# One layer of an RWKV-7 and neighbourhood-attention backbone: a gate's matmuls moved into the fourth inverse's first steps, residual halves of w_out and m made by adding DMAs, and the first half's sums written ahead of the second modulation

## The chip, the cores and the metric

The kernel runs on one core of a Trainium2 chip. The metric is the device time of one execution in microseconds (us). Engines are named as the profile names them: PE is the matrix engine (PEld its weight loads), DVE the vector engine, ACT the scalar engine, POOL the general engine, SP the engine that issues most DMAs.

## What is computed

640 tokens (128 of a prompt, 512 of a latent grid) go through one layer of width 1024. The lines that matter here are

```python
o_rw, s_new = _rwkv_branch(...)      # 8 heads, forward and backward, gated state recurrence
o_na = _na_context(q, k, v)  or  _na_latent(q, k, v, ctx_k, ctx_v, p["na_rpb"])
merged = (jax.nn.sigmoid(gate_rw) * (o_rw @ p["w_o_rwkv"])
          + jax.nn.sigmoid(gate_na) * (o_na @ p["w_o_na"]))
x = x + g1 * (merged @ p["w_out"])
h2 = _rmsnorm(x, p["norm2_g"]) * (1.0 + sc2) + sh2
x = x + g2 * ((jax.nn.silu(h2 @ p["ffn_w1"]) * (h2 @ p["ffn_w3"])) @ p["ffn_w2"])
```

All of it is in float32 accuracy. The kernel gets it by splitting each operand of the large matmuls into a high part `hi` (rounded to the PE's fast 32-bit form) and a residual `lo` (value minus `hi`), and adding three products: hi by hi, lo by hi, hi by lo.

## The kernel before

The layer is one stream in time. First come the norm and the modulation vectors, then the projections, the neighbourhood attention, the RWKV recurrence, the merge, `w_out`, and from about 745 us to the end the feed-forward part (FFN).

**The recurrence** works in four groups of chunks, `ct` = 0 to 3. Each group has four stages: `main`, `inv`, `carry` and `out`. `inv(ct, S)` (L1253) inverts 32 by 32 triangles on DVE in 30 steps `s` (L1274 for the first three, then a product L1288 and a sum L1292, each in two halves). After certain steps it calls jobs: `PRM["jobs"][ct]` names the steps after which `v_job` (L1211, small transposes of v), `t_job` (L1234) and `g_job` (L1183, L1186, small products) are put on PE, each job for a part of the chunks' slots. A `g_job` leaves a closure `masks`, which multiplies its results by a triangular mask on DVE (L1195 into `AG`, L1198 into `TG`); `PRM["mds"][ct]` names the steps after which the closures run. All these small products, and those of the bonus term (`bonus`: L1103, L1117, L1132 on PE; L1107, L1134, L1439, L1440, L1443 on DVE), write into one rotating pool of six PSUM banks named `w`. A product that opens a bank waits until whoever read the bank's previous tenant has finished.

**The fill.** The recurrence alone leaves PE idle, so `weave` (L1552) pulls matmuls of another stream, `stream(PRM["order"])`, between the steps. The first number of each entry of `PRM["plan"]` says how many of the stream's matmuls follow a step; the other two advance `out` of the group before and `bonus`. In the inverse of ct=3 the stream has reached the last gate, g14 (L572, tiles `h` times a gate weight, `fl`), and then a0, the first products with the recurrence's outputs of earlier groups, whose operands `o` come back from DRAM by eight DMAs at L1476 (320 KB each, `o<-o_d`). Gate weights come by DMA from SP (`wst`, L164 or L167) and are split by `wcast`: ACT casts `hi` (L177); `lo` is made either by DVE (L179, `wst - hi`) or, for the tiles marked so, by ACT writing minus the rounded value into `lo` (L175) and POOL issuing a DMA that adds `wst` to it (L176, an adding or accumulating DMA).

**The merge and w_out.** `last_gen` (L1634) makes the merged `m`, 8 blocks of 128 columns in 2 halves of 320 tokens, 16 halves in all. Each takes three matmuls (L1644), a DVE operation that combines them with the gate (L1645, reading PSUM), a DVE sum with the other branch (L1647), an ACT cast to `mh` (L1648) and a POOL subtraction to `ml` (L1649). From the sixth half on, two matmuls of `w_out`'s first half of columns (`w_out_gen`, L288, results `acc`) follow each half, and the rest are drained after the last.

**After w_out's first half.** `add_gated` (L1680) multiplies `acc` by the gate row `G` (L1683, result `tt`) and adds it to the residual `x2` (L1684), for five token tiles. The second modulation turns two rows into columns by 16 tiny matmuls (`pc`, L1704) and three small DVE operations (L1706 to L1708). Then PE runs w_out's second half of columns (L288 again); its weights' `lo` parts are DVE's L179.

Inside the regions marked manual the order of an engine is the order of the code; PE is manual throughout the part around `last_gen`, the other engines are not there, and a scheduler at build time fixes their order.

Of the kernel before, what the change touches and what calls it, by code (L numbers as in the profile page):

```python
# [14 lines left out]
P = 128  # L15
# [34 lines left out]
        ("0.0.0 16.1.0 8.1.1 9.0.0 2.1.0 8.1.1 13.1.1 0.1.1 0.1.1 0.1.1 0.1.0 6.1.0 6.1.0 6.1.0 6.1.0 "  # L50
         "6.1.0 6.1.0 7.1.0 6.0.0 6.0.0 6.0.0 6.0.0 6.0.0 6.0.0 7.0.0 6.0.0 6.0.0 6.0.0 6.0.0 6.0.0 "
         "6.0.0 6.0.0 11.0.0 8.0.0 8.0.0 2.0.0 0.0.0"),
# [15 lines left out]
        "w >hb >lb",  # L68
        ""),
    fp=(6, 12, 18), h2e="dpddddpddd", x0e="a", ze="aa", y2=1, y1=0, sc=3, sr=3, sp=1, mg=1.915, h1=0.952,  # L70
    h2=0.91, jobs=((2, 9, 28), (2, 9, 28), (2, 9, 28), (2, 8, 28)),
    mds=((4, 12), (4, 12), (4, 12), (4, 12)), bud=((1.8, 0.8), (1.3, 1.8)), off=6, tk=2, h3=1,
    h4=1.07, g1=2, km="dddddddd", kb="ddpd", ma="d", yo="pppd", r0="pd", rl=(0, 0, 0), lh=(0, 0, 1, 1),
    wl="dddddddddppppppppppppppppppppppppppdddd", nu=9, lg=14, jo=(2, 0, 1), na=(
        "6.0.12.0.1 6.0.12.0.0 6.0.12.0.0 6.0.12.0.2 6.0.12.0.0 6.0.12.0.2 6.0.12.0.0 6.0.12.0.2 6.0.12.0.0 "
        "6.0.12.0.2 6.0.12.1.0 6.1.12.1.2 6.2.12.2.0 6.1.12.2.2 6.0.12.2.0 6.1.12.1.2 6.2.14.2.0 "
        "6.2.14.1.2 6.2.14.2.0 6.2.14.2.0 6.3.18.2.0 10.0.10.0.0"))
# [30 lines left out]
def body(ctx: ExitStack, tc: tile.TileContext, xs, xp, cols, consts, w_ada, b_row, w_rw, w_qkv,  # L108
# [73 lines left out]
    def wload(src, eng=None):  # L182
        return wcast(wdma(src), eng)
# [307 lines left out]
    pend, off, hold = [], [0], [False]  # L491
# [580 lines left out]
    with ExitStack() as s3:  # L1072
# [500 lines left out]
        with tc.manual_schedule(engines=FIRST):  # L1573
            for d in range(2):
                akr(S, d)
            pool.memset(Nt, 0.0)
            og = iter(())
            for ct in range(4):
                bg = bonus(ct, S)
                weave(main(ct, S), (og,))  # L1580
                if ct == 0:
                    for d in range(2):
                        r_(S, d, dve)
                    pool.memset(Rt, 0.0)
                marks.add(f"A{ct}")
                S2 = Ct()
                if ct < 3:
                    prep_dma(ct + 1, S2, sb.tile([P, NT], F32, tag="mx", bufs=2, name=nm("upw")))
                weave(inv(ct, S), (og, bg))
                drain(og)  # L1590
                marks.add(f"I{ct}")
                if ct < 3:
                    need(f"k{ct + 1}")
                    prep_cast(S2)
                    pg = prep(ct + 1, S2)
                else:
# [24 lines left out]
                hold[0] = True  # L1621
                weave(carry(ct, S, last), (pg,), PRM["bud"])
                hold[0] = False
                og = out(ct, S)
                S = S2
            weave(og)
            need(*(f"b{i}" for i in range(4)))
            c0 = wload(w_out[0])


    pp = open_pool(ctx, "pp4", bufs=3, space=PSUM)
# [1 line left out]
    mh, ml = hilo("m")  # L1633
    def last_gen():  # L1634
        ts_ = []
        for c8 in range(8):
            t = pre_t() if c8 < 4 else trp.tile([P, NT], F32, tag="tr", bufs=4, name=nm("tr"))
            sp.dma_start(t, trw_d[c8])
            ts_.append(t)
        for c8, t in enumerate(ts_):  # L1640
            for (a, b) in halves:
                ps = pp.tile([P, 512], F32, tag="tp", name=nm("fl"))
                for n, (w, x) in enumerate(((wo[0], o3[0]), (wo[0], o3[1]), (wo[1], o3[0]))):
                    pe.matmul(ps[:, :H2], w[:, c8 * 128:c8 * 128 + 128], x[:, a:b], start=n == 0, stop=n == 2)  # L1644
                dve.scalar_tensor_tensor(out=t[:, a:b], in0=t[:, a:b], scalar=1.0, in1=ps[:, :H2],  # L1645
                                         op0=ALU.add, op1=ALU.mult)
                dve.tensor_tensor(out=t[:, a:b], in0=mt[c8][:, a:b], in1=t[:, a:b], op=ALU.add)  # L1647
                act.copy(mh[:, c8, a:b], t[:, a:b])  # L1648
                pool.tensor_tensor(out=ml[:, c8, a:b], in0=t[:, a:b], in1=mh[:, c8, a:b].bitcast(F32),  # L1649
                                   op=ALU.subtract)  # L1650
                yield

    def w_out_gen(pss, ws, toks, **kw):
        return tok_gen(pss, pp, (mh, ml), ws, list(range(8)), toks, **kw)

    pss = {}
    trp = open_pool(hs, "trp")
    weights(hs, 2, 2)
    w0 = w_out_gen(pss, [c0] + [w_out[q] for q in range(1, 4)], range(5))
# [5 lines left out]
    hs.close()  # L1665
    nstack.close()
    xpool = open_pool(ctx, "xpool")
    x2 = [xpool.tile([P, 1024], F32, name=f"x2_{i}") for i in range(5)]
    G = xpool.tile([P, 2, 1024], F32, name="G")
    m2 = xpool.tile([P, 24, 2], F32, name="m2")[:, 0:8, :]  # L1670
    s2 = xpool.tile([P, 8, 2], F32, name="s2")
    for i in range(5):
        sp.dma_start(x2[i], xs[i * 128:(i + 1) * 128, :] if i < 4 else xp)

    def load_gate(b):
        ad = adr[:, :]
# [32 lines left out]
    for i in range(5):  # L1709
        add_gated(pss[i], i, 0, 0.5)  # L1710


    nr = [{} for _ in range(5)]
# [372 lines left out]
```

## Time and profile before

| | |
|---|---|
| median of 3 runs | 1182.05 us (1181.28 to 1182.42) |
| profiled execution | 1182.22 us, of it span 1180.4 us |
| granted PE clock, mean | 0.99 |
| PE busy | 1123.0 us, 95% of the span |
| DVE, ACT, POOL busy | 777.8, 531.6, 192.1 us |
| DMA moved | 148.11 MB, mean 125 GB/s |

The span is the time between the first and the last recorded instruction; 1.8 us of the execution lie around it. A row of the timeline gives the start, the time until the row's last instruction ended, engine, line, operation, output and input tiles, and in square brackets the idle time ahead of it and what ended that.

### The profile page before, as it was taken

To read this page: it belongs to the slowest core of one execution; us is meant where nothing else is said; L and a number is where in the kernel's file an instruction comes from. 1 tells how busy PE (TensorE), PEld (TensorE's weight loads), DVE (VectorE), ACT (ScalarE), POOL (GpSimd) and SP (SyncE) were. 2 spreads that over 40 slices of the span, in tenths; PEclk is the share of its full clock that TensorE was granted. 3 is DMA by queue.
4 is the path that set the end of the run, shared out by engine and by line. 5 is a ranking of instruction groups with operands and counts; after the bars stand their busy time and mean duration, and the time that the engine had idled before them with its cause. 6 is when DMAs were issued, how large, how long until landed. Compare 5 with 4: busy or idle time off the path is not lost.

```text
span 1180.4 us, 26871 instructions
## 1 busy us (share of the span) xinstructions
PE 1123.0 (95%) x11160; PEld 995.3 (84%) x11160; DVE 777.8 (66%) x1635; ACT 531.6 (45%) x1050; POOL 192.1 (16%) x260
## 2 busy tenths in 40 slices
PE   6999999899999999999799899999999999999998
PEld 4688877789888988888698777899899989998997
DVE  4565465559558747936486756887568757775775
ACT  4444656554564665556343323554124422441330
POOL 1162244320101202111100141100000000001000
PEclk9999999999999999999899999999999999999999
DMA  9752777654433523433753641312312231232122
GB/s 334 261 116 86 240 224 227 208 137 109 104 83 93 138 69 91 112 102 95 241 151 102 223 161 54 108 54 90 107 54 90 79 101 55 89 107 90 54 79 101
DMA packets 60194, 148.11 MB, mean 125 GB/s; under 512 B 7428, under 2 KB 22404, under 8 KB 60072
## 3 DMA queue, kind: packets, MB, share of 16 engines
q1 hardware_dynamic: 55464, 131.56, 34.1%
q0 software_dynamic: 3744, 13.63, 5.9%
q8 instruction: 88, 1.44, 0.5%
q10 hardware_dynamic: 864, 1.20, 0.3%
q14 instruction: 34, 0.28, 0.1%
HBM read 118.41 MB, written 14.32 MB: 112 GB/s over the span
## 4 chain that ended last, share of the span: by engine, by line
PE 62%; DVE 9%; ACT 3%; issue 3%; DMA 1%; SPq 0%; POOL 0%; DVEq 0%; ACTq 0%; POOLq 0%
PE f L1805 21%; PE acc L288 16%; PE fl L201 12%; PE w L1362 1%; PE w L1389 1%; DVE pr L1288 1%; PE w L1402 1%; DMA o<-o_d 1%; PE w L1374 1%; PE mm L201 1%; PE w L1186 1%; DVE RL L1292 1%; PE w L1380 1%; PE w L1419 1%; PE w L1234 1%
## 5 line engine op out<-in xcount | busy, mean ns | idle before, releaser
L1805 PE MATMUL f<-t,whi 128*128 128x320 f32 x640 | 141.8, 310 | 0.0
L1805 PE MATMUL f<-b,whi 128*128 128x320 f32 x608 | 136.2, 311 | 2.0 <-ACT b L189 1.7
L288 PE MATMUL acc<-whi,u 128*128 128x512 f32 (+1 forms) x448 | 136.0, 385 | 0.0
L201 PE MATMUL fl<-h,whi 128*128 128x320 f32 x672 | 121.2, 320 | 1.3 <-issue 1.3
L177 ACT CAST whi<-wst 128x1024 fp32r<-128x1024 f32 (+1 forms) x77 | 79.2, 1033 | 63.6 <-PE acc L288 43.0
L1805 PEld LDWEIGHTS f<-t,whi 128*128 128x128 f32 x640 | 107.3, 189 | 0.0
L201 PEld LDWEIGHTS fl<-h,whi 128*128 128x128 f32 x672 | 101.4, 188 | 6.1 <-issue 1.4
L1805 PEld LDWEIGHTS f<-b,whi 128*128 128x128 f32 x608 | 102.3, 189 | 3.2 <-ACT b L189 2.1
L1805 PE MATMUL f<-t,wlo 128*128 128x320 f32 x320 | 99.1, 310 | 0.0
L288 PEld LDWEIGHTS acc<-whi,u 128*128 128x128 f32 x448 | 83.5, 188 | 16.6
L1805 PE MATMUL f<-b,wlo 128*128 128x320 f32 x304 | 94.6, 311 | 2.2 <-DVE wlo L1849 2.2
L1846 ACT CAST whi<-ws 128x1024 fp32r<-128x1024 f32 x40 | 42.0, 1051 | 108.7 <-PE f L1805 47.5
L179 DVE TENSOR_TENSOR wlo<-wst,whi 128x1024 fp32r<-128x1024 f32 (+1 forms) x51 | 62.2, 1227 | 38.1 <-ACT whi L177 37.5
L288 PE MATMUL acc<-wlo,u 128*128 128x512 f32 (+1 forms) x224 | 86.3, 385 | 0.0
L1860 POOL TENSOR_TENSOR ws<-wst 128x512 f32<-128x512 f32 x20 | 28.1, 1405 | 340.7 <-DVE wlo L1849 226.7
L288 PE MATMUL acc<-whi,h 128*128 128x512 f32 x240 | 78.1, 399 | 0.9 <-DVE h L413 0.9
L201 PE MATMUL fl<-h,wlo 128*128 128x320 f32 x336 | 63.4, 321 | 0.0
L1683 DVE SCALAR_TENSOR_TENSOR tt<-acc,G 128x512 f32<-128x512 f32 (+1 forms) x51 | 34.5, 679 | 42.8 <-PE acc L288 42.7
L1846 ACT CAST whi<-wst 128x1024 fp32r<-128x1024 f32 (+1 forms) x48 | 41.4, 870 | 42.3 <-PE acc L288 37.6
L1805 PEld LDWEIGHTS f<-t,wlo 128*128 128x128 f32 x320 | 60.2, 188 | 0.0
L1805 PEld LDWEIGHTS f<-b,wlo 128*128 128x128 f32 x304 | 57.5, 189 | 2.5 <-DVE wlo L1849 2.5
L1849 DVE TENSOR_TENSOR wlo<-ws,whi 128x1024 fp32r<-128x1024 f32 x40 | 54.9, 1372 | 6.3 <-ACT whi L1846 6.3
(342 smaller groups left out, 2503.7 us busy)
## 6 DMA issues: line engine op xcount, KB each, us to landing
wst<-in_w_dram SPq DMA_DIRECT2D x66, 512.0 KB
wst<-in_w_rw_dram SPq DMA_DIRECT2D x31, 512.0 KB
wlo<-wst POOLq DMA_DIRECT2D x26, 512.0 KB, 4.6
wa<-in_w_ada_dram SPq DMA_DIRECT2D x24, 512.0 KB
f<-in_w_ada_dram SPq DMA_DIRECT2D x16, 512.0 KB
wst<-in_w_qkv_dram SPq DMA_DIRECT2D x12, 512.0 KB
o<-o_d SPq DMA_DIRECT2D x14, 320.0 KB
x<-in_xs_dram SPq DMA_DIRECT2D x8, 512.0 KB
```

The costliest lines, as they stand in the source:

```text
L177: act.copy(hi[:, :n], st[:, :n])
L179: dve.tensor_tensor(out=lo[:, :n], in0=st[:, :n], in1=hi[:, :n].bitcast(F32), op=ALU.subtract)
L201: pe.matmul(ps[:, :t1 - t0], w[:, a:a + 128], x[:, k0 + kt, t0:t1], start=n == 0, stop=n == 3 * nk - 1)
L288: pe.matmul(pss[i][:, a:b], lhs(x, kt, ts_), w[:, cs_], start=ki == 0 and n == 0, stop=ki == last and n == 2)
L1186: pe.matmul(pr[h][hrows[h ^ i], o_], x[hrows[h], :], R_[hrows[h], l, :], start=True, stop=True)
L1234: pe.matmul(pt[h][hrows[h ^ i], o_], S.BK[l // 10][hrows[h], l % 10, i, :], idh(h), start=True, stop=True)
L1288: dve.tensor_tensor(out=prv, in0=V(RL[:, s + 1 + a, :], [[32, b - a], [0, s]], s), in1=V(RL[:, s, :], [[0, b - a], [1, s]]), op=ALU.mult)
L1683: dve.scalar_tensor_tensor(out=tt, in0=ps[:, a:b], scalar=c, in1=G[:, g, sl], op0=ALU.mult, op1=ALU.mult)
L1805: pe.matmul(ps[:, :H2], w_[:, c_], x_[:, kt, :], start=first and kt + n == 0, stop=last and kt == 3 and n == 2, skip_group_check=more)
L1846: act.copy(r[0][:, :width], src())
L1849: dve.tensor_tensor(out=r[1][:, :width], in0=src(), in1=r[0][:, :width].bitcast(F32), op=ALU.subtract)
L1860: eng_x(PRM["se"][i - 1]).tensor_tensor(out=o_, in0=x, in1=y, op=op)
```

## The change

Six edits, in the order of the program:

1. In the inverse of ct=3 the plan puts 56 fill matmuls (g14's 48 with a0's first ones) after the first four steps as 20, 12, 12, 12, where they were 16, 8, 9, 2, 8, 13 over six.
2. In the same inverse the first job moves from step 2 to step 4, its masks from step 4 to step 7, and the second job's masks from step 12 to step 13.
3. The `lo` parts of w_out's first two weight tiles are made by ACT and an adding DMA in place of DVE's L179.
4. `m`'s `lo` parts lose their 16 POOL subtractions. For blocks 1 to 5 ACT writes minus the rounded value and, after the second half of the block, one adding DMA of 320 KB adds the value. For blocks 0, 6 and 7 DVE subtracts (L1654 of the new file, two halves each).
5. `G` gets its place and its loads ahead of the loads of `x2`.
6. The five `add_gated` of the first half are written ahead of the second modulation.

```diff
-        ("0.0.0 16.1.0 8.1.1 9.0.0 2.1.0 8.1.1 13.1.1 0.1.1 0.1.1 0.1.1 0.1.0 6.1.0 6.1.0 6.1.0 6.1.0 "
+        ("0.0.0 20.1.0 12.1.1 12.0.0 12.1.0 0.1.1 0.1.1 0.1.1 0.1.1 0.1.1 0.1.0 6.1.0 6.1.0 6.1.0 "
...
-    h2=0.91, jobs=((2, 9, 28), (2, 9, 28), (2, 9, 28), (2, 8, 28)),
-    mds=((4, 12), (4, 12), (4, 12), (4, 12)), bud=((1.8, 0.8), (1.3, 1.8)), off=6, tk=2, h3=1,
+    h2=0.91, jobs=((2, 9, 28), (2, 9, 28), (2, 9, 28), (4, 8, 28)),
+    mds=((4, 12), (4, 12), (4, 12), (7, 13)), bud=((1.8, 0.8), (1.3, 1.8)), off=6, tk=2, h3=1,
...
-            c0 = wload(w_out[0])
+            c0 = wload(w_out[0], pool)
...
-                pool.tensor_tensor(out=ml[:, c8, a:b], in0=t[:, a:b], in1=mh[:, c8, a:b].bitcast(F32),
-                                   op=ALU.subtract)
+                if c8 in PRM["md"]:
+                    act.activation(ml[:, c8, a:b], t[:, a:b], AF.Copy, scale=-1.0)
+                    if a:
+                        pool.dma_start(ml[:, c8, :].bitcast(F32), t, accum_op=ALU.add)
+                else:
+                    dve.tensor_tensor(out=ml[:, c8, a:b], in0=t[:, a:b], in1=mh[:, c8, a:b].bitcast(F32),
+                                      op=ALU.subtract)
...
-    w0 = w_out_gen(pss, [c0] + [w_out[q] for q in range(1, 4)], range(5))
+    w0 = w_out_gen(pss, [c0, wload(w_out[1], pool)] + [w_out[q] for q in range(2, 4)], range(5))
...
+    G = xpool.tile([P, 2, 1024], F32, name="G")
     x2 = [xpool.tile([P, 1024], F32, name=f"x2_{i}") for i in range(5)]
-    G = xpool.tile([P, 2, 1024], F32, name="G")
...
+    load_gate(4)
+    for i in range(5):
+        sp.dma_start(x2[i], xs[i * 128:(i + 1) * 128, :] if i < 4 else xp)
...
-    load_gate(4)
+    for i in range(5):
+        add_gated(pss[i], i, 0, 0.5)
```

How the instructions stand, at three places.

**SP, in the inverse of ct=3.** Rows are DMAs in the order in which SP issues them: `wst` is the last weight tile but one of the w_o blocks, `o10` and `o00` the operands of a0, `tna_d` the gate's result going out. Before:

```order
L164 DMA wst_1031_7721<-in_w_o_dram 128x2x512
L1476 DMA o10_7598<-o_d1_81 128x640
L1476 DMA o00_7596<-o_d0_80 128x640 x2
L1476 DMA o10_7598<-o_d1_81 128x640
L1476 DMA o00_7596<-o_d0_80 128x640
L1476 DMA o10_7598<-o_d1_81 128x640
L1476 DMA o00_7596<-o_d0_80 128x640
L1476 DMA o10_7598<-o_d1_81 128x640
L581 DMA tna_d_78<-fl_1034_7731 128x320
```

After:

```order
L1476 DMA o10_7598<-o_d1_81 128x640
L1476 DMA o00_7596<-o_d0_80 128x640 x2
L1476 DMA o10_7598<-o_d1_81 128x640
L1476 DMA o00_7596<-o_d0_80 128x640
L1476 DMA o10_7598<-o_d1_81 128x640
L1476 DMA o00_7596<-o_d0_80 128x640
L1476 DMA o10_7598<-o_d1_81 128x640
L164 DMA wst_1023_7645<-in_w_o_dram 128x2x512
L581 DMA tna_d_78<-fl_1026_7653 128x320
```

The weight tile's load has moved from ahead of the eight loads to behind them.

**DVE, in the inverse of ct=3**, from step 5 (the rows with 65 elements) to the bonus rows after step 7 (84 elements). Before, the first job's masks stand ahead of step 5:

```order
L1195 TENSOR_TENSOR AG_2886<-w_1027_7644,K_67 64x4x64 x2
L1198 TENSOR_TENSOR TG_2890<-w_1028_7645,K_67 128x4x64
L1198 TENSOR_TENSOR TG_2890<-w_1029_7646,K_67 128x4x64
L1288 TENSOR_TENSOR pr_1021_7590<-RL_1016_7554 128x65 x2
L1292 TENSOR_TENSOR RL_1016_7554<-RL_1016_7554,pr_1021_7590 128x13x5 x2
L1134 TENSOR_TENSOR bv_993_7321<-w_1030_7708,vp0_623 128x320
```

After, they stand behind step 7, and so behind L1134, L1439 and L1440:

```order
L1134 TENSOR_TENSOR bv_993_7321<-w_1037_7738,vp0_623 128x320
L1288 TENSOR_TENSOR pr_1021_7594<-RL_1016_7554 128x72
L1288 TENSOR_TENSOR pr_1021_7594<-RL_1016_7554 128x78
L1292 TENSOR_TENSOR RL_1016_7554<-RL_1016_7554,pr_1021_7594 128x12x6
L1292 TENSOR_TENSOR RL_1016_7554<-RL_1016_7554,pr_1021_7594 128x13x6
L1439 TENSOR_TENSOR out_1006_7437<-out_1006_7437,w_1038_7744 128x512
L1440 TENSOR_TENSOR out_1006_7437<-out_1006_7437,w_1039_7745 128x128
L1288 TENSOR_TENSOR pr_1021_7594<-RL_1016_7554 128x84 x2
L1292 TENSOR_TENSOR RL_1016_7554<-RL_1016_7554,pr_1021_7594 128x12x7 x2
L1195 TENSOR_TENSOR AG_2886<-w_1034_7704,K_67 64x4x64 x2
L1198 TENSOR_TENSOR TG_2890<-w_1035_7705,K_67 128x4x64
```

The first number behind `w` is the bank's turn: w_1040, which PE opens with its second L1132, is the sixth after w_1034, which the masks of L1195 read. On PE the order is before: g14's first half, job 1, g14's second half with the first L1132 inside it, a0's twelve matmuls, L1117, the second L1132, job 2; and after: g14 whole, a0's twelve, job 1, the first L1132, L1117, the second L1132, job 2.

**DVE, after w_out's first half**: the modulation's three rows, the gated products `tt`, the sums `x2`, and the splits `wlo` of w_out's second half. Before:

```order
L1706 COPY s2_9373<-pc_1227_9402 128x16
L1707 TENSOR_SCALAR m2_9372<-pc_1227_9402 128x16
L1708 TENSOR_TENSOR m2_9372<-m2_9372,C_68 128x16
L1683 SCALAR_TENSOR_TENSOR tt_1230_9426<-acc_1202_9135,G_9371 128x512
L1683 SCALAR_TENSOR_TENSOR tt_1231_9429<-acc_1203_9136,G_9371 128x512
L1684 TENSOR_TENSOR x2_0_9366<-x2_0_9366,tt_1230_9426 128x512
L1684 TENSOR_TENSOR x2_1_9367<-x2_1_9367,tt_1231_9429 128x512
L1683 SCALAR_TENSOR_TENSOR tt_1232_9432<-acc_1204_9137,G_9371 128x512
L1683 SCALAR_TENSOR_TENSOR tt_1233_9435<-acc_1205_9138,G_9371 128x512
L1684 TENSOR_TENSOR x2_2_9368<-x2_2_9368,tt_1232_9432 128x512
L1684 TENSOR_TENSOR x2_3_9369<-x2_3_9369,tt_1233_9435 128x512
L179 TENSOR_TENSOR wlo_1243_9473<-wst_1241_9470,whi_1242_9472 128x1024
```

After:

```order
L1716 TENSOR_TENSOR m2_9379<-m2_9379,C_68 128x16
L1690 SCALAR_TENSOR_TENSOR tt_1227_9409<-acc_1205_9145,G_9373 128x512
L1690 SCALAR_TENSOR_TENSOR tt_1228_9412<-acc_1206_9146,G_9373 128x512
L1691 TENSOR_TENSOR x2_0_9374<-x2_0_9374,tt_1227_9409 128x512
L1690 SCALAR_TENSOR_TENSOR tt_1229_9415<-acc_1207_9147,G_9373 128x512
L1691 TENSOR_TENSOR x2_1_9375<-x2_1_9375,tt_1228_9412 128x512
L1690 SCALAR_TENSOR_TENSOR tt_1230_9418<-acc_1208_9148,G_9373 128x512
L1691 TENSOR_TENSOR x2_2_9376<-x2_2_9376,tt_1229_9415 128x512
L1690 SCALAR_TENSOR_TENSOR tt_1231_9421<-acc_1209_9149,G_9373 128x512
L1691 TENSOR_TENSOR x2_3_9377<-x2_3_9377,tt_1230_9418 128x512
L1691 TENSOR_TENSOR x2_4_9378<-x2_4_9378,tt_1231_9421 128x512
L179 TENSOR_TENSOR wlo_1243_9480<-wst_1241_9477,whi_1242_9479 128x1024
```

The modulation's rows still come first in both. The third product has one sum less ahead of it, and wlo_1243 stands behind ten rows of the sums where it stood behind eight.

On DVE in `last_gen`, one L179 (before: two) is left ahead of the first L1645, and two L1654 of block 0 stand behind the first six L1645 and six L1647.

More of the change, by code (lines that the diff above doesn't have):

```diff
@@ L49 @@
         "22.2 0.0 4.0 6.0",
-        ("0.0.0 16.1.0 8.1.1 9.0.0 2.1.0 8.1.1 13.1.1 0.1.1 0.1.1 0.1.1 0.1.0 6.1.0 6.1.0 6.1.0 6.1.0 "
-         "6.1.0 6.1.0 7.1.0 6.0.0 6.0.0 6.0.0 6.0.0 6.0.0 6.0.0 7.0.0 6.0.0 6.0.0 6.0.0 6.0.0 6.0.0 "
-         "6.0.0 6.0.0 11.0.0 8.0.0 8.0.0 2.0.0 0.0.0"),
[3 rows of a table added]
         ("10.0 0.0 6.1 4.2 0.0 6.1 4.2 0.0 6.1 4.2 0.0 6.1 4.2 0.0 6.1 4.2 0.0 6.1 4.2 0.0 6.1 4.2 0.0 "
@@ L70 @@
     fp=(6, 12, 18), h2e="dpddddpddd", x0e="a", ze="aa", y2=1, y1=0, sc=3, sr=3, sp=1, mg=1.915, h1=0.952,
-    h2=0.91, jobs=((2, 9, 28), (2, 9, 28), (2, 9, 28), (2, 8, 28)),
-    mds=((4, 12), (4, 12), (4, 12), (4, 12)), bud=((1.8, 0.8), (1.3, 1.8)), off=6, tk=2, h3=1,
+    h2=0.91, jobs=((2, 9, 28), (2, 9, 28), (2, 9, 28), (4, 8, 28)),
+    mds=((4, 12), (4, 12), (4, 12), (7, 13)), bud=((1.8, 0.8), (1.3, 1.8)), off=6, tk=2, h3=1,
     h4=1.07, g1=2, km="dddddddd", kb="ddpd", ma="d", yo="pppd", r0="pd", rl=(0, 0, 0), lh=(0, 0, 1, 1),
-    wl="dddddddddppppppppppppppppppppppppppdddd", nu=9, lg=14, jo=(2, 0, 1), na=(
+    wl="dddddddddppppppppppppppppppppppppppdddd", nu=9, md=(1, 2, 3, 4, 5), lg=14, jo=(2, 0, 1), na=(
         "6.0.12.0.1 6.0.12.0.0 6.0.12.0.0 6.0.12.0.2 6.0.12.0.0 6.0.12.0.2 6.0.12.0.0 6.0.12.0.2 6.0.12.0.0 "
@@ L1667, in body @@
     xpool = open_pool(ctx, "xpool")
+    G = xpool.tile([P, 2, 1024], F32, name="G")
     x2 = [xpool.tile([P, 1024], F32, name=f"x2_{i}") for i in range(5)]
-    G = xpool.tile([P, 2, 1024], F32, name="G")
     m2 = xpool.tile([P, 24, 2], F32, name="m2")[:, 0:8, :]
     s2 = xpool.tile([P, 8, 2], F32, name="s2")
-    for i in range(5):
-        sp.dma_start(x2[i], xs[i * 128:(i + 1) * 128, :] if i < 4 else xp)
     def load_gate(b):
@@ L1708, in body @@
     dve.tensor_tensor(out=m2, in0=m2, in1=V(C[:, :], [[1, 8], [0, 2]], CO["n2"]), op=ALU.mult)
-    for i in range(5):
-        add_gated(pss[i], i, 0, 0.5)
     nr = [{} for _ in range(5)]
```

2 rows, old and new, of the table plan are left out of this document.

## The prediction

> **What bounds the kernel now.** I read the shares first, then the waits, then the timelines of the three stretches that the change touches.
>
> ```profile
> span 1180.4 us, 26871 instructions
> ...
> PE 1123.0 (95%) x11160; PEld 995.3 (84%) x11160; DVE 777.8 (66%) x1635; ACT 531.6 (45%) x1050; POOL 192.1 (16%) x260
> ...
> PE 62%; DVE 9%; ACT 3%; issue 3%; DMA 1%; SPq 0%; POOL 0%; DVEq 0%; ACTq 0%; POOLq 0%
> ```
>
> PE is busy for 95% of the span and holds 62% of the chain that ended last. PE's matmuls stay the same in number and size, so the change can win only PE's idle time in these stretches, or time at a low clock, and lose by adding some. The first stretch is the inverse of ct=3, 553 to 586 us.
>
> ```profile
> DVE out L1439 <- PE w L1117: 12.6, 1, 12.6
> ...
> PE fl L201 <- DMA o<-o_d: 7.7, 7, 2.9
> ```
>
> The columns are the wait in total, how often, and the longest. PE waits 7.7 us for a0's operands, and DVE, whose order is fixed here, stands 12.6 us behind L1117, which PE runs after a0. This is the largest single stall near the change.
>
> **Edits 1 and 2: the inverse of ct=3.** The rows of SP, POOL and PE (start, length) say when the operands were asked for and used.
>
> ```profile
> 562.53 0.38 SPq L164 DMA_DIRECT2D wst<-in_w_o_dram  x1
> 563.01 4.73 SPq L1476 DMA_DIRECT2D o<-o_d  x8
> ```
> ```profile
> 557.97 0.86 POOL L176 DMA_DIRECT2D wlo<-wst  x1 [0.35 <-ACT whi L177]
> ...
> 567.60 0.92 POOL L176 DMA_DIRECT2D wlo<-wst  x1 [5.65 <-ACT wlo L175]
> ```
> ```profile
> 557.94 1.17 PE L1103 MATMUL w<-K,pre 128*128 128x2 f32 x10
> ...
> 560.32 0.27 PE L1211 MATMUL w<-K,vp 64*64 64x64 f32 x2
> ...
> 562.10 0.42 PE L572 MATMUL fl<-h,whi 128*128 128x320 f32 x1
> ...
> 576.78 0.64 PE L201 MATMUL fl<-o,whi 128*128 128x320 f32 x1 [1.11 <-DMA o<-o_d]
> ...
> 578.28 1.27 PE L1117 MATMUL w<-K,pre 128*128 128x128 f32 x5
> 579.35 1.27 PE L1132 MATMUL w<-bv,K 128*128 128x320 f32 x2
> 580.55 1.10 PE L1211 MATMUL w<-K,vp 64*64 64x64 f32 x26
> ```
> ```profile
> 564.00:566.00 2.00, 1.84 (x11) 1.37 (x9) 0.43 (x3) 0.52 (x2) 0.00 (x0) 1.00 1.00 375
> ...
> 570.00:572.00 2.00, 0.80 (x2) 0.47 (x2) 0.00 (x0) 0.00 (x0) 0.00 (x0) 0.65 0.94 327
> ```
>
> The window's last three columns are the granted clock, the DMA share and GB/s. Before, `wst` waited on SP until 562.53 (its buffer is read by the adding DMA issued at 557.97), and the eight loads stood behind it. Now they stand ahead of it and need only that g14's first half is done, about 558.5 (the 24 matmuls now run without L1103 among them). Issue thus moves from 563.01 to about 558.65, 4.36 us earlier, and 0.5 MB of `wst` no longer goes first: at 375 GB/s 1.4 us. But the loads now share the engines with that adding DMA, and with the one issued at 567.60 before, which moves forward too; I take 1.0 us back. The last operand then comes at 576.78 - 4.36 - 1.4 + 1.0 = 572.0 and a0 ends 1.5 us later (as from 576.78 to 578.28), at 573.5. Bounds: 571 (no sharing lost) to 575.5 (the rate of the stretch is no better than before and sharing costs 3 us).
>
> A gain of 4.8 us at this point does not reach job 2, because job 1 and its masks now lie in the gap. DVE's rows price them:
>
> ```profile
> 562.10 0.86 DVE L1195 TENSOR_TENSOR AG<-w,K 64x256 f32<-64x256 f32 x2 [0.44 <-PE w L1183]
> ...
> 565.73 0.49 DVE L1134 TENSOR_TENSOR bv<-w,vp 128x320 f32<-128x320 f32 x1 [1.56 <-PE w L1132]
> 566.13 0.37 DVE L1288 TENSOR_TENSOR pr<-RL 128x72 f32<-128x72 f32 x2
> 566.42 0.37 DVE L1292 TENSOR_TENSOR RL<-RL,pr 128x72 f32<-128x72 f32 x2
> ...
> 579.38 0.69 DVE L1439 TENSOR_TENSOR out<-out,w 128x512 f32<-128x512 f32 x1 [12.58 <-PE w L1117]
> 579.98 0.28 DVE L1440 TENSOR_TENSOR out<-out,w 128x128 f32<-128x128 f32 x1
> 580.18 0.40 DVE L1288 TENSOR_TENSOR pr<-RL 128x84 f32<-128x84 f32 x2
> 580.49 0.40 DVE L1292 TENSOR_TENSOR RL<-RL,pr 128x84 f32<-128x84 f32 x2
> ```
>
> The second L1132 opens the bank that L1195 must first read, so PE waits for a chain that starts when a0 ends: job 1, 1.78 (560.32 to 562.10); the first L1132, 0.60 (half of 579.35 to 580.55); then DVE's L1134 0.45, step 6 0.66, L1439 0.60, L1440 0.20, step 7 0.71 and L1195 0.78; then the second L1132 0.60. Together 6.38: job 2 starts at 579.9 where it started at 580.55, **-0.65**; with the bounds of a0's end -3.1 to +1.4. PE is idle from L1117's end to L1195's, 3.40 - 1.07 = 2.33 us: the chain's 0.45 to 0.78 sum to 3.40, and L1117 covers 1.07 of it. Queued behind the waiting L1132 is all of job 2; behind that, PE is full. On DVE the masks' 1.5 us move and are not added; `inv` on DVE is then about 0.7 us earlier, which PE can't use.
>
> The low clock is the open price: 0.65 granted in 570 to 572 above, after the idle time. Idle of 2.33 us could lower it again for job 2. That costs between nothing and 1.5 us (job 2 takes 4.45 us, much of it waiting on ACT). I take nothing, since the idle must fall into one window, and keep 1.5 for the range.
>
> The Trainium skill, page "TensorE: Matmul & The Clock Gate", section "Why this matters for your kernels", advises against idle gaps of over about 3 us, one window of idle time bringing half rate. By that rule 2.33 us would cost nothing. The next part's 2.46 us of idle time was followed by a low clock, so here the measurement is the stricter, and the 1.5 us stay in the range.
>
> **Edits 3 and 4: last_gen.** PE's, DVE's and the window's rows:
>
> ```profile
> 668.67 1.47 PE L1644 MATMUL fl<-o,f 128*128 128x320 f32 x9
> 672.60 2.44 PE L1644 MATMUL fl<-o,f 128*128 128x320 f32 x9 [2.46 <-DVE pre L1645]
> 674.85 1.19 PE L288 MATMUL acc<-whi,m 128*128 128x512 f32 x2
> ```
> ```profile
> 669.80 2.35 DVE L179 TENSOR_TENSOR wlo<-wst,whi 128x1024 fp32r<-128x1024 f32 x2
> 672.07 1.27 DVE L1645 SCALAR_TENSOR_TENSOR pre<-pre,fl 128x320 f32<-128x320 f32 x3
> ...
> 676.25 2.00 DVE L1647 TENSOR_TENSOR pre<-mt,pre 128x320 f32<-128x320 f32 x3
> ```
> ```profile
> 672.00:676.00 4.00, 3.40 (x12) 2.97 (x13) 4.00 (x10) 1.29 (x4) 1.68 (x2) 0.63 0.79 252
> ```
> ```profile
> PE fl L1644 <- DVE tr L1645: 1.6, 2, 0.9
> ```
>
> One of the two L179 ahead goes (1.13), so PE's second group starts about 1.1 us earlier. But the second `acc` matmul needs block 0's `lo`, now behind six L1645 and six L1647 on DVE: from 670.9, twelve at 0.42 is 676.0, where POOL had it ready for a matmul at about 675.4. So PE loses 0.7 there and is idle 2.9 us before it. After that DVE is lighter: L1647 beside POOL took 0.67 on average in the row above and takes about 0.42 with POOL's 16 subtractions gone, and six subtractions at 0.45 come on. PE's two later stalls (1.6 us) go. With the clock low again after the idle time the end of w_out's first half moves by -0.55; with it full, -2.05. I take **-0.55**, nearest to the 2.46 us row with its 0.63, and keep -2.05. The other end: block 1's `lo` is an adding DMA.
>
> ```profile
> wlo<-wst POOLq DMA_DIRECT2D x26, 512.0 KB, 4.6
> ```
>
> Issued about 675.9, it lands 4.6 us later if it is like the median of these (the 320 KB may take less), 680.5, and is needed about 681.7. Two more microseconds of landing time make PE wait 1 us; so +1.0 is the upper end. Edit 3's first tile is split long before its use, at no cost while ACT (1.3 busy in 4 us above) has room. The accumulations' issue on POOL costs nothing, since POOL has nothing else to do there.
>
> **Edits 5 and 6: after w_out's first half.**
>
> ```profile
> 714.62 0.73 PE L288 MATMUL acc<-whi,m 128*128 128x512 f32 x2 [0.73 <-DVE tt L1683]
> ...
> 717.91 0.39 PE L288 MATMUL acc<-wlo,m 128*128 128x512 f32 x1
> ```
> ```profile
> 711.49 1.28 DVE L1683 SCALAR_TENSOR_TENSOR tt<-acc,G 128x512 f32<-128x512 f32 x2
> ...
> 716.29 1.21 DVE L179 TENSOR_TENSOR wlo<-wst,whi 128x1024 fp32r<-128x1024 f32 x1
> ```
>
> The sums' text moves ahead, but the order of DVE keeps the modulation first, so no start is gained there. `tt` of the third tile ends 0.60 us earlier, which shortens PE's wait at 714.62. But wlo_1243 now has ten rows of 0.60 ahead where it had eight: it ends at 718.7 instead of 717.5, and PE, which used it at 717.91 and would now want it at 717.3, waits until 718.75: **+0.85**. Bounds: 0 (PE late by as much from elsewhere) to +1.5 (the split after it late too). G's earlier load costs nothing: it was there before its use.
>
> **Sum.** -0.65 - 0.55 + 0.85 = -0.35 on the profiled execution of 1182.22 (span 1180.4 and 1.8 around it), 1181.9; the median of the runs is 0.2 lower, so **1181.7**.
>
> **The rivals.**
> - *Faster: the chain of masks isn't the gate.* The operands come at 569.5, a0 ends at 571, and the 2.9 us of idle time in last_gen straddle two windows. Then -3.1 - 2.05 + 0.85 = -4.3, 1177.8. For it: 375 GB/s in one window above. Against: 327 GB/s with the adding DMA under way. If no bank held the L1132 the gain would be 4.8, and the time 1177.5.
> - *Slower: PE waits for the masks.* Place: the second L1132. If a0 ends after 574.2, job 2 starts later than before; at 575.5 it is +1.4, with the low clock +1.5 more, and with block 1's DMA late +1.0 and +0.85 after it: +4.75, 1186.8. It decides from a0's end at 574.2 or from a clock that drops at both gaps.
> - *The sums aren't moved at all.* Then edit 6 is only the reordering of two sums and a split. The order says so, and the forecast contains it. Were `tt` instead ready at pc's start, PE's waits of about 1.9 us would go, and the time would be 1179.
>
> **How the numbers follow.** Forecast, 1179.5 to 1184: 0.42. Faster rival, up to 1179.5: 0.31. Slower rival, 1184.4 to 1187: 0.24. Sums ready early: 0.03. About 0.2%, 2.4 us, is what a measurement of this kernel can tell from no change: faster is under 1179.7, slower over 1184.4. Faster is 0.31 and 0.03 and 0.03 of the forecast, 0.37; slower 0.24 and 0.04 of it, 0.28; the same 0.35. The range from 1176.8 to 1186.5 leaves out the last tenth of each rival.
>
> **What would show it.** In the changed profile: the eight `o` loads at about 558.7 ahead of `wst`; a0 ending near 573.5; a wait of PE's second L1132 for DVE's L1195 of about 2.3 us, and job 2 near 579.9; no L179 pair ahead of the first L1645 but a wait of `acc` for DVE's L1654; wlo_1243 named as what PE waits for near 718. The forecast is wrong if job 2 starts before 578, if the clock is low in job 2, or if PE waits on the adding DMAs of `m`.

## The result, and the profile after

The changed kernel takes 1186.15 us, the median of 11 runs, against 1182.42 of 11 runs of the kernel before on the same chips. The ratio is 1.003 with a 95% interval of 1.0018 to 1.0043: slower by 2.1 to 5.1 us. The forecast was 1181.7, a gain of 0.35. The time lies inside the range (1176.8 to 1186.5), at its upper edge, and the sign is wrong.

The profiled execution of the changed kernel (1184.87 us) is among its quickest, so its trace shows less than the whole loss. Its first lines of the page:

```profile
span 1183.1 us, 26884 instructions
...
PE 1123.0 (95%) x11160; PEld 993.9 (84%) x11160; DVE 773.7 (65%) x1639; ACT 537.8 (45%) x1062; POOL 180.8 (15%) x251
```

PE is busy for the same 1123.0 us in a span that is 2.7 us longer, so in sum the trace's loss is idle time on PE. To find it I compare not the clock times of the two traces, which drift apart by 1 us before the change begins, but the distance between marks that both have. The first mark is DVE's L1257, which opens the inverse of ct=3, and the second is PE's first L1448, which follows job 2. Before:

```profile
555.50 1.25 DVE L1257 STREAM_TRANSPOSE RL<-Nt 128x1024 f32<-128x1024 f32 x1 [2.76 <-ACT Nt L1169]
```
```profile
585.00 0.81 PE L1448 MATMUL w<-lg__620,gup 128*128 128x320 f32 x2
```

After, the same two marks and some of PE's rows between them:

```profile
554.48 1.25 DVE L1257 STREAM_TRANSPOSE RL<-Nt 128x1024 f32<-128x1024 f32 x1 [2.75 <-ACT Nt L1169]
```
```profile
572.29 0.64 PE L201 MATMUL fl<-o,whi 128*128 128x320 f32 x1 [3.41 <-DMA o<-o_d]
...
573.92 0.37 PE L1211 MATMUL w<-K,vp 64*64 64x64 f32 x2
...
577.11 1.29 PE L1132 MATMUL w<-bv,K 128*128 128x320 f32 x2
578.24 0.71 PE L1117 MATMUL w<-K,pre 128*128 128x128 f32 x5
578.98 0.81 PE L1132 MATMUL w<-bv,K 128*128 128x320 f32 x2
580.16 0.97 PE L1211 MATMUL w<-K,vp 64*64 64x64 f32 x26 [0.38 <-DVE out L1439]
...
585.40 0.81 PE L1448 MATMUL w<-lg__620,gup 128*128 128x320 f32 x2
```

From mark to mark it was 29.50 and is 30.92: +1.42. Two windows of the changed kernel (the third number from the end is the granted clock):

```profile
571.00:574.00 3.00, 1.71 (x9) 1.38 (x11) 0.00 (x0) 0.00 (x0) 0.00 (x0) 0.50 1.03 337
574.00:577.00 3.00, 3.00 (x96) 2.99 (x96) 0.00 (x0) 1.33 (x5) 0.00 (x0) 0.50 1.04 407
```

Job 1 (573.92 to 577.11) now falls into the time at half clock that the wait for the operands leaves behind it. SP's and POOL's rows show the loads and the second adding DMA:

```profile
557.55 5.80 SPq L1476 DMA_DIRECT2D o<-o_d  x8
563.53 0.38 SPq L164 DMA_DIRECT2D wst<-in_w_o_dram  x1
```
```profile
564.07 0.92 POOL L176 DMA_DIRECT2D wlo<-wst  x1 [2.55 <-ACT wlo L175]
```

In last_gen and after w_out's first half PE's waits are now these:

```profile
672.14 1.58 PE L1644 MATMUL fl<-o,f 128*128 128x320 f32 x9 [1.33 <-DVE pre L1645]
...
676.95 0.67 PE L288 MATMUL acc<-whi,m 128*128 128x512 f32 x1 [2.61 <-DVE m L1654]
...
714.64 0.73 PE L288 MATMUL acc<-whi,m 128*128 128x512 f32 x2 [0.27 <-DVE tt L1690]
...
719.62 0.50 PE L288 MATMUL acc<-wlo,m 128*128 128x512 f32 x1 [1.49 <-DVE wlo L179]
```

The stretches between marks, before and after, in us (the marks are those two, the start of PE's first L1644, DVE's row `COPY s<-pc`, and PE's first product of the FFN that waits for ACT b L189):

| stretch | before | after | difference |
|---|---|---|---|
| inverse: L1257 to L1448 | 29.50 | 30.92 | +1.42 |
| L1448 to last_gen | 83.67 | 83.94 | +0.27 |
| last_gen and w_out's first half | 42.43 | 42.26 | -0.17 |
| from there to the FFN's first wait | 34.25 | 35.70 | +1.45 |
| FFN to the end of the span | 435.05 | 435.80 | +0.75 |

The whole, 2.7, is these 3.7 less the 1.0 by which this execution happened to be early at the first mark.

The last row goes with the clock, and with no instruction that the edits change. The FFN begins with a wait of PE for ACT (1.71 us before, 1.78 after), and in one execution the clock falls low behind it and in another it doesn't. The same window, before and after:

```profile
748.00:751.00 3.00, 3.00 (x23) 3.00 (x22) 2.31 (x5) 2.50 (x5) 0.54 (x1) 1.00 0.57 224
```
```profile
748.00:751.00 3.00, 3.00 (x14) 3.00 (x15) 2.93 (x7) 0.88 (x2) 0.00 (x0) 0.63 0.13 45
```

Of the 17 traces kept here, eleven have a low clock that begins within 2 us of the end of that wait, and take 435.6 to 435.8 us from there to the end. The other six, the kernel before among them, have it some 33 us later and take 435.0 to 435.1.

### The profile page after: what moved, and what is told of

The parts are those of the page before. It is cut to its first block, busy times and chain, and to the rows that moved or that the text cites. A ratio compares the mean times of both kernels' runs of the same rounds, so it can differ in the third digit from the quotient of the medians.

```text
span 1183.1 us, 26884 instructions
## 1 busy us (share of the span) xinstructions
PE 1123.0 (95%) x11160; PEld 993.9 (84%) x11160; DVE 773.7 (65%) x1639; ACT 537.8 (45%) x1062; POOL 180.8 (15%) x251
## 3 DMA queue, kind: packets, MB, share of 16 engines
q8 instruction: 88, 1.44, 0.5%
## 4 chain that ended last, share of the span: by engine, by line
PE 46%; DVE 3%; DMA 1%; issue 1%; ACT 1%; SPq 0%; DVEq 0%; POOLq 0%; ACTq 0%
PE f L1811 21%; PE acc L288 17%; PE fl L201 3%; DMA o<-o_d 1%; DMA wlo<-wst 1%; DVE hq L1770 0%; DVE t L190 0%; PE fl L1644 0%; SPq L1476 0%; PE xt L1740 0%; PE w L1362 0%; PE w L1186 0%; DVE x L1691 0%; PE w L1402 0%; PE w L1234 0%
## 5 line engine op out<-in xcount | busy, mean ns | idle before, releaser
L179 DVE TENSOR_TENSOR wlo<-wst,whi 128x1024 fp32r<-128x1024 f32 (+1 forms) x49 | 59.6, 1222 | 41.4 <-ACT whi L177 40.8
```

What stands on the lines that cost most here:

```text
L179: dve.tensor_tensor(out=lo[:, :n], in0=st[:, :n], in1=hi[:, :n].bitcast(F32), op=ALU.subtract)
```

## The experiments

Theory A: the inverse loses because job 1 and its masks stand in the gap that the earlier operands open; the loss after w_out comes from DVE's late split; last_gen is about even. The rivals stand with each run. Each kernel is compared with runs of the kernel before on the same chip, as a ratio with its 95% interval. Differences between two changed kernels are those of their ratios, times 1182 us; they carry some 1.5 to 2 us of uncertainty, so beside them stand the stretches of the traces, which repeat to a few tenths where the clock is the same.

**Each pair of edits alone.** Edits 1 and 2 alone (the diff's first two pieces):

> The kernel before with edits 1 and 2 alone (the fill's plan and the jobs and masks of the fourth inverse). Theory A (job 1 and its masks now stand between a0 and job 2, so the operands' earlier arrival is spent on them, at half the clock): slower than before by about 1.4 us, ratio 1.001, with a0 ending near 574 and job 2 starting no earlier than before. Rival B (the inverse gains, as the changed trace read against its own start would allow if 1.0 us of it is chance, and the loss is all behind it): same or faster by 0.5 to 1 us.

1186.41 us, ratio 1.0038 (1.0023 to 1.0052): 4.5 us slower where 1.4 was expected. The inverse's stretch is 30.34, +0.84, and a0 ends 19.2 us after the mark, nearly as in the changed kernel (19.4). So the inverse does lose; rival B falls. The time says more than the trace's stretch. The rest of the profiled one lies in stretches whose code is as before: +0.50 ahead of last_gen, +1.10 in last_gen (43.53 in place of 42.43), +0.56 after it and +0.73 in the FFN. In last_gen PE waits longer once, where the kernel before waited 0.92:

```profile
683.43 1.04 PE L1644 MATMUL fl<-o,f 128*128 128x320 f32 x3 [1.88 <-DVE tr L1645]
```

Three times the clock falls to 0.50 where it doesn't in the trace of before: from 683.8 to 687, right behind this wait, from 714 to 718 and from 748 to 752. Why it does is left open.

Edits 3 and 4 alone:

> The kernel before with edits 3 and 4 alone (adding DMAs for two tiles of w_out and five blocks of m, DVE for the other three blocks). Theory A (the wait for block 0's residual on DVE takes the place of the wait for the split, the later stalls go): between 0.6 us faster and 0.5 us slower. Rival C (the idle time at block 0 drops the clock in most executions, and the changed kernel's lower mean clock comes from here): slower by 1 to 2 us.

1182.71 us, ratio 1.0006 (0.999 to 1.0022). Even, as theory A had it, though the interval, from 1.2 us faster to 2.6 slower, doesn't exclude rival C by itself. The stretch is 42.23, -0.20, and the clock falls low in it once, as before. Its waits are as in the changed kernel:

```profile
670.12 1.59 PE L1644 MATMUL fl<-o,f 128*128 128x320 f32 x9 [1.33 <-DVE pre L1645]
...
674.92 0.66 PE L288 MATMUL acc<-whi,m 128*128 128x512 f32 x1 [2.62 <-DVE m L1654]
```

Edits 5 and 6 alone:

> The kernel before with edits 5 and 6 alone (G and its loads first, sums written ahead of the second modulation). Theory A (the split wlo_1243 comes two sums later on DVE and PE waits for it): slower by 0.9 to 1.5 us, with PE waiting for DVE wlo L179 once by about 1.5 us. Rival D (that wait is absorbed by the FFN's first wait for ACT): same within 0.3 us.

1183.86 us, ratio 1.0018 (1.0006 to 1.0029). The stretch after w_out is 35.69, +1.44 to before, and the wait is there without the other edits:

```profile
712.80 0.74 PE L288 MATMUL acc<-whi,m 128*128 128x512 f32 x2 [0.27 <-DVE tt L1684]
...
717.78 0.50 PE L288 MATMUL acc<-wlo,m 128*128 128x512 f32 x1 [1.47 <-DVE wlo L179]
```

Rival D falls: the FFN's wait for ACT is 1.78 against 1.71 and doesn't take it up. The order of the instructions says which of the two edits it is; neither was run alone. With edit 6 alone the order on PE, DVE and SP is that of the kernel before, to the row; with edit 5 alone DVE's order is that of both edits. So writing the sums ahead does nothing to these orders, and giving G its place and loads first is what makes the scheduler put all the sums ahead of the split.

The three pairs' losses add up to 7.3 us (4.5, 0.7 and 2.1), and the whole change loses 3.5. The difference, 3.8, is a little more than the uncertainty of such a sum, about 3.3 if the runs are independent, so the times don't show that the pairs add. In the traces the edited stretches of the pairs give +0.84 - 0.20 + 1.44 = 2.08, against 2.70 in the changed kernel.

**Job 1 and its masks.** The changed kernel with

```diff
-    (2, 9, 28), (4, 8, 28)), mds=(... (7, 13))
+    (2, 9, 28), (2, 8, 28)), mds=(... (4, 13))
```

> The changed kernel with edit 2 undone but for the second masks (first job back at step 2, its masks at step 4, second masks at step 13), the plan and the order of SP's loads as changed. Theory A (job 1 and its masks in the gap cost what the loads gain): faster than the changed kernel by 3 to 4 us, about 1182 to 1183, and job 2 starts near 577. Rival B (the loads' arrival is the gate all the same): no more than 1 us faster than the changed kernel.

1180.27 us, ratio 0.9982 (0.9971 to 0.9993): 5.7 us faster than the changed kernel, with the same loads in the same order on SP. Its row of the mark on DVE, and PE's rows:

```profile
555.27 1.25 DVE L1257 STREAM_TRANSPOSE RL<-Nt 128x1024 f32<-128x1024 f32 x1 [2.76 <-ACT Nt L1169]
```
```profile
570.97 0.63 PE L201 MATMUL fl<-o,whi 128*128 128x320 f32 x1 [0.18 <-DMA o<-o_d]
571.40 1.27 PE L201 MATMUL fl<-o,wlo 128*128 128x320 f32 x4
572.47 1.27 PE L1132 MATMUL w<-bv,K 128*128 128x320 f32 x2
...
575.80 1.41 PE L1211 MATMUL w<-K,vp 64*64 64x64 f32 x26
...
580.56 0.81 PE L1448 MATMUL w<-lg__620,gup 128*128 128x320 f32 x2
```

The stretch is 25.29, 5.63 less than in the changed kernel. Behind a0's end (572.47) L1448 follows after 8.1 us in place of 11.5. And a0 itself ends 17.2 us after the mark in place of 19.4: here the second adding DMA goes out 11.6 us after the mark (566.82) and there 9.6 (564.07), so the loads run longer without it. Theory A holds, and the gain is more than the 3 to 4 us expected.

The masks moved, job 1 left behind a0 (`mds` (5, 13) in the changed kernel):

> The changed kernel with the first job's masks after step 5 in place of step 7 (job 1 still at step 4, behind a0). Theory A1 (what costs is job 1's own place: it runs at half the clock between a0 and L1132, 3.2 us long, and nothing that DVE does can start before): 0 to 1.5 us faster than the changed kernel, 1184.5 to 1186. Rival A2 (what costs is the masks' place behind the bonus rows): nearly all of the 5.9 us that moving both back gave, 1181 or less.

1184.48 us, ratio 1.0018 (1.0007 to 1.0029), 1.4 faster than the changed kernel, within the uncertainty; the stretch is 29.57, 1.35 less, of the 5.63 that moving both back gives. Of the 1.35, a0's end is 0.42 and the way from there to job 2 0.89. Job 2 itself takes 5.20 us in place of 5.24. It no longer waits for L1195, but for DVE's second L1134:

```profile
583.02 0.38 PE L1186 MATMUL w<-R__2889,f 64*64 64x64 f32 x9 [1.10 <-DVE bv L1134]
```

So by the stretches the masks' place is at most a quarter, and job 1's place, with what it does to the DMAs, the rest: theory A1. Job 1 at step 2 with the masks left late was not run.

**How much hangs on a0's end.** The changed kernel as it is, with the two weight tiles whose adding DMAs run beside the loads split by DVE (`wl`: two letters p to d):

> The changed kernel as it is (job 1 behind a0), with the two tiles whose adding DMAs run beside the operands' loads split by DVE. Theory A (a0's end gates job 1, the masks and job 2, and the adding DMAs hold a0's end back): a0 ends 2 us earlier and everything behind it too, 1184 to 1184.5 against the 1186.15 of the changed kernel, still slower than before. Rival (the low clock in job 1 is what matters, and a0's end does not): no change, 1186.

1182.36 us, ratio 0.9992 (0.998 to 1.0005): 4.5 faster than the changed kernel, more than expected, and not to be told from before. The mark on DVE and PE's rows:

```profile
558.14 1.25 DVE L1257 STREAM_TRANSPOSE RL<-Nt 128x1024 f32<-128x1024 f32 x1 [2.75 <-ACT Nt L1169]
```
```profile
573.08 0.63 PE L201 MATMUL fl<-o,whi 128*128 128x320 f32 x1 [1.61 <-DMA o<-o_d]
573.51 1.27 PE L201 MATMUL fl<-o,wlo 128*128 128x320 f32 x4
574.71 0.37 PE L1211 MATMUL w<-K,vp 64*64 64x64 f32 x2
...
585.24 0.81 PE L1448 MATMUL w<-lg__620,gup 128*128 128x320 f32 x2
```

The last operand is used 14.9 us after the mark in place of 17.8, and the stretch is 27.10, 3.82 less. Job 1 still takes 3.0 us (574.71 to the L1132 at 577.70), at half clock. So a0's end counts in full and the rival falls. One more thing differs: SP issues the weight tile's load ahead of the eight again, as in the kernel before:

```profile
560.59 0.38 SPq L164 DMA_DIRECT2D wst<-in_w_o_dram  x1
```

The loads are asked for 3.1 us after the mark, as in the changed kernel (561.21 and 557.55). So the 2.9 us are the gain without the adding DMAs and with this load ahead; what the adding DMAs cost by themselves was not run. Their cost overlaps with that of job 1's place. Moving job 1 and masks back takes 5.63 off the stretch, the splits by DVE 3.82, and both together, in a run further down (23.17), 7.75.

**The plan alone, and the other costs.** The kernel before with edit 1 and `mds` (4, 13), job 1 at step 2:

> The kernel before with edit 1 and the second masks at step 13 alone: job 1 stays at step 2. Theory A (the plan, which lets SP ask for the operands 4 to 5 us earlier, is worth 4.2 us as long as job 1 is not put behind a0): 1178 against 1182.1, job 2 starting about 4.5 us after the trace's mark before it earlier than before. Rival (the gain of the kernel with job 1 at step 2 came from edits 3 and 4): 1181 to 1182.

1181.02 us, ratio 0.9978 (0.9963 to 0.9992), 2.6 us faster (0.9 to 4.4) where 4.2 was expected; the stretch is 25.71, 3.79 less than before. The absolute time is the rival's, but the kernel before took 1183.04 beside these runs. The plan and the order of the loads gain without edits 3 and 4, so the rival falls.

With edits 3 and 4 added, which makes the kernel of 1180.27 less edits 5 and 6:

> The kernel before with edit 1 (the plan), the second masks at step 13, and edits 3 and 4; job 1 at step 2, edits 5 and 6 left out. Theory A (the sums' order on DVE costs 1.5 us by itself): 1178.5 to 1179, 1.5 us faster than with edits 5 and 6 in (1180.27). Rival D (their cost is absorbed when the inverse is short): within 0.5 us of 1180.3.

1179.1 us, ratio 0.9978 (0.9964 to 0.9991), 0.5 less than with edits 5 and 6. That is inconclusive: 1.5 and nothing are both within the uncertainty. One reason shows in its trace, a wait of PE that the changed kernel doesn't have:

```profile
680.17 0.47 PE L288 MATMUL acc<-whi,m 128*128 128x512 f32 x1 [1.48 <-DMA m<-pre]
```

That is block 1's adding DMA, issued at 672.91. Block 1 by DVE (`md` without 1):

> The kernel with job 1 at step 2, without edits 5 and 6 (1179.1), and block 1's residual by DVE in place of its adding DMA. Theory A (its trace's wait of 1.48 us for that DMA is a cost of edit 4 that shows when last_gen starts earlier): that wait goes, about 1 us faster, 1178.1. Rival (the DVE rows put in its place delay the next halves as much): same within 0.5 us.

1177.7 us, ratio 0.9954 (0.9936 to 0.9973). The wait is gone, and the time falls by 2.8. That is more than the 1.5 of the wait, but the 1.3 between them lie within the uncertainty.

The two tiles of the inverse split by DVE in the kernel of 1179.1:

> The kernel with job 1 at step 2, without edits 5 and 6 (1179.1), with the two weight tiles whose adding DMAs run beside the eight loads of operands split by DVE instead. Theory A (the loads, asked for 5.5 us earlier, gain less because the adding DMAs share the engines): the last operand lands about 2 us earlier, a0 and job 2 follow, 1 to 2 us faster. Rival (the loads' own bytes set their end): the last operand lands within 0.5 us of the same time, no gain.

1176.95 us, ratio 0.9945 (0.9927 to 0.9963), 3.9 less where 1 to 2 us were expected; the stretch is 23.17 in place of 24.86, 1.69 less. The other 2.2 us are about as large as the uncertainty.

**More adding DMAs.** w_out's fifth and sixth tile by adding DMAs, in the kernel of 1180.27:

> The kernel with job 1 back at step 2 and all other edits (1180.27), and the residual halves of w_out's fifth and sixth tile made by ACT and adding DMAs, so that neither stands on DVE behind the sums. Theory A (PE's wait near 718 is the late split wlo_1243, and the wait near 675 is DVE's work ahead of block 0's residual): the wait for L179 near 718 goes, 1.5 us, and the wait for L1654 shrinks by about 1.1 us: 1178. Rival: the DMAs land late and PE waits for them instead, same or slower.

1183.69 us, ratio 1.001 (0.9997 to 1.0023): a miss, 3.3 slower than the kernel that it was to mend. The wait for L179 at 718 and most of that for L1654 go, and others come: 1.95 us for block 1's adding DMA, 0.98 for that of a tile, 0.53 for another L179, and this one in PE's rows:

```profile
722.46 0.73 PE L288 MATMUL acc<-whi,m 128*128 128x512 f32 x2 [0.90 <-ACT whi L177]
```

The fifth tile alone, in the kernel of 1179.1:

> As the kernel with job 1 at step 2 and without edits 5 and 6, and w_out's fifth tile split by an adding DMA: no L179 is left ahead of last_gen on DVE. Theory A (DVE's queue ahead of block 0's residual is PE's wait in last_gen): the wait for L1654 falls from 2.6 to about 1.5 us, the time by about 1 us against the same kernel without it. Rival C (last_gen is set by the clock after that idle time and by the products after it): no difference.

1181.1 us, ratio 0.9992 (0.9981 to 1.0004): 1.7 us slower, a miss too. PE's wait for L1654 is 1.06, less than expected, but PE's and POOL's rows show

```profile
680.12 0.47 PE L288 MATMUL acc<-whi,m 128*128 128x512 f32 x1 [4.29 <-DMA m<-pre]
```
```profile
669.70 0.86 POOL L176 DMA_DIRECT2D wlo<-wst  x1 [2.53 <-ACT wlo L175]
672.09 0.86 POOL L1652 DMA_DIRECT2D m<-pre  x1 [1.53 <-DVE pre L1645]
```

Block 1's DMA stands behind the tile's, 2.4 us after it, and its result is used 8.0 us after its issue. The same with block 1 by DVE:

> The kernel with w_out's fifth tile by an adding DMA (1181.1, where PE waited 4.29 us for block 1's adding DMA), with block 1's residual by DVE. Theory A (the adding DMAs of the tiles and of m share one queue and engines, and block 1's lands 8 us after its issue): the 4.29 us wait goes, 3 to 4 us faster, 1177.5 to 1178. Rival (the next block's adding DMA is waited for instead): 1180 to 1181.

1177.72 us, ratio 0.9955 (0.9934 to 0.9976). The 4.29 us are gone and the time is 4.4 less; theory A holds, the next block isn't waited for. But the tile itself has gained nothing by the times: the same kernel without it took 1177.7.

**A version that beats both.** Job 1 at step 2, no edits 5 and 6, both tiles and block 1 by DVE:

> Job 1 at step 2, edits 5 and 6 left out, the two tiles of the inverse split by DVE, and block 1's residual by DVE. Theory A (the three costs are separate places): the gains add, 1176.95 less the 1.4 us of block 1, 1175 to 1176. Rival (with the operands early PE is the bound and block 1's wait is hidden): 1177, as without block 1's change.

1176.2 us, ratio 0.9942 (0.9925 to 0.9958). Whether the gains add can't be told from 1176.95 with these intervals. With the fifth tile of w_out by an adding DMA as well:

> As the kernel with all three mends, and w_out's fifth tile by an adding DMA. Theory A: its L179 ahead of last_gen goes, 1 us less: 1174 to 1175. Rival (the adding DMAs queue behind one another, as block 1's did): no gain or slower, 1176 or more.

1172.75 us, ratio 0.9918 (0.9897 to 0.9938), 9.7 us under the kernel before. That the tile brings 2.8 of it is not shown: the uncertainty is some 3 us, with six runs of 1171.2 to 1176.6, and beside block 1 by DVE alone the tile gave nothing. PE's largest waits in last_gen are then 1.07 for L1654 and 1.05 for a tile's adding DMA.

## Why the prediction was wrong, step by step

**The failed step is the inverse's term, -0.65.** In distances from the mark it reads: a0 ends 4.8 earlier, the chain behind it is 4.1 longer (6.38 against 2.27), job 2 as long as before. Measured: a0's end 19.44 after the mark against 22.78, 3.34 earlier; the chain 6.24 (573.92 to 580.16), 3.97 longer; job 2 and what follows to L1448 5.24 in place of 4.45, +0.79. The sum is +1.42.

- *a0's end.* The sum gave back 1.0 us for the adding DMAs beside the loads. The run with both taken off DMA has the last operand 2.9 us earlier, with the weight tile's load ahead. Part of that was there before, too; to come out right the 1.0 had to be about 2.4. The bound named for it (sharing 3 us) was nearer than the value taken.
- *The clock in absolute times.* The forecast 573.5 for a0's end looks met by 573.92, but this trace is 1.0 early at the mark. Only the distance shows the miss.
- *Job 1 at 1.78.* That row was taken where the clock was full. Moved behind waits for the operands it ran at 0.50 and took 3.19. The first L1132 was taken as half of its row, 0.60. The whole row (x2) is one call of L1132, and at half clock it took 1.13 (577.11 to 578.24).
- *The bank.* The second L1132 doesn't wait for L1195: it ran at 578.98, and L1195 at 580.96. Its bank isn't the one that L1195 reads; counting six turns back gave the wrong one, and which one it is stays open.

```profile
580.96 0.86 DVE L1195 TENSOR_TENSOR AG<-w,K 64x256 f32<-64x256 f32 x2
```

 What waits for DVE is job 2: 0.38 us for L1439 ahead of it, and 0.6 for L1195 within it.

```profile
PE w L1234 <- DVE AG L1195: 0.6, 1, 0.6
```

 The chain came out nearly right as a sum by luck, for errors that cancel: job 1 and the first L1132 were 1.9 us too short together, and the 3.40 us of DVE's rows, thought to stand between the first L1132 and the second, did not hold PE there (0.74 passed). Job 2's +0.79 is in good part that wait: PE's waits in it are 0.56 for L1195 and 0.36 to which the trace gives no cause, against 0.23 before. Moving the masks to step 5 didn't win it back: there job 2 waits for L1134 and is as long. The clock wasn't low in job 2: it was 1.00 from 580 on.

**last_gen, -0.55.** Right in mechanism and nearly in size: PE's wait for L1654 was 2.61 where 2.9 was worked out, the later stalls are gone, the stretch is -0.17, and edits 3 and 4 alone are even. PE didn't wait for block 1's adding DMA in the changed kernel, but not because it landed in the 4.6 us that the forecast took. The DMA rows of the changed kernel have 7.2 as the median of blocks 1 to 3:

```profile
m<-pre POOLq DMA_DIRECT2D x3, 320.0 KB, 7.2
```

 Here the clock fell low behind the wait for L1654 (677 to 681), and PE came to block 1 late enough. In the trace of the kernel of 1179.1 it stayed at 1.00 there and PE waited 1.48; with the fifth tile's adding DMA ahead it waited 4.29. So the rival's last piece is a real cost that this execution happened not to pay.

**After w_out, +0.85.** Right mechanism, too small: +1.45 in the trace. The split starts 0.37 later (718.35) than ten rows of 0.60 after 711.98 would have it, since a product and a sum in turn take about 1.3 us for the pair in this order, and 1.2 in the one before:

```profile
713.89 0.69 DVE L1690 SCALAR_TENSOR_TENSOR tt<-acc,G 128x512 f32<-128x512 f32 x1
714.50 0.68 DVE L1691 TENSOR_TENSOR x<-x,tt 128x512 f32<-128x512 f32 x1
715.22 0.69 DVE L1690 SCALAR_TENSOR_TENSOR tt<-acc,G 128x512 f32<-128x512 f32 x1
...
718.35 2.35 DVE L179 TENSOR_TENSOR wlo<-wst,whi 128x1024 fp32r<-128x1024 f32 x2
```

The earlier `tt` gave PE 0.46 (0.73 to 0.27) for the 0.60 worked out. PE's waits make 1.49 - 0.46 = 1.03 of the 1.45; the other 0.4 has no wait that names it. And the text put the blame on both edits, where the order alone shows it is G's.

**The rivals.** The slower one asked for a0's end after 574.2 and got it: 19.44 after the mark is 574.9 on the clock of the trace before. It put its chance at 0.24. Its place, the second L1132, was wrong like the forecast's. The faster one asked for the last operand at 569.5, 14.0 after the mark. Only kernels without the adding DMAs beside the loads come near it, with 14.2 to 14.9.

**What the FFN adds** (+0.75 in the trace) was not forecast, and comes from where the low clock falls in the profiled execution, as the 17 traces show. No run shows it to be a cost of the edits.

## What to carry to other kernels

Work that is moved behind a wait takes on the clock of that wait: price it with a row from a stretch that has been idle, not from where it used to stand. An operand that is asked for earlier arrives earlier only by what the transfers beside it leave (4.4 us earlier asked, 3.5 earlier used, here), so look for which other DMAs move with it. And where a scheduler sets an engine's order, read the order: moving the text of the sums left DVE's order as it was, and moving a tile and its loads changed it.

## What the runs showed of the hardware

- Low clock also falls on places whose code is unchanged, in one execution and not in another. The window of 229 to 232 us in the trace of before:

```profile
229.00:232.00 3.00, 3.00 (x15) 3.00 (x14) 2.02 (x8) 1.97 (x6) 1.63 (x2) 0.55 0.58 186
```

and the same in that of the changed kernel:

```profile
229.00:232.00 3.00, 3.00 (x25) 2.81 (x27) 2.02 (x9) 2.32 (x7) 1.29 (x2) 1.00 0.58 180
```

 Runs of one kernel spread over some 5 us here (1181.28 to 1186.15 for the kernel before), so a loss of 3 us took many runs to see. The Trainium skill, page "TensorE: Matmul & The Clock Gate", section "Part 1: The HAM clock gate (the "warmup" mystery)", says that the window of the gate is free-running and that the point of transition depends on where in it the work falls. These traces agree.
- What a wait of PE does to the clock differs from one execution to the next: the FFN's first wait of 1.7 to 1.8 us is followed within 2 us by 0.50 in eleven of the 17 traces and not in six. With it there the FFN is about 0.7 us longer (435.7 against 435.1). In the changed kernel the low stretch is some 3.4 us long: windows of 1 us from 748 were granted 0.90, 0.50, 0.50, 0.50, 0.90.
- An adding DMA beside others is slow to land: 8.0 us from issue to use in the kernel where a tile's adding DMA of 512 KB went out 2.4 us ahead. For the 320 KB of `m` the median in the changed kernel was 7.2 (blocks 1 to 3), against 4.6 for the 512 KB tiles in the kernel before. Why the smaller ones took longer is not shown.
